# Hybrid attention and recurrence layer: the input norm's loads, squares, weight splits and first projection block in another order

## The chip, the cores and the metric

One Trainium2 chip, one core of it. The metric is the device time of one execution in microseconds, the median of the runs. A time belongs to the whole layer, of which the change touches the first part.

## The reference, cut to what matters

```
h = concat([meta (16 tokens), x (1024 tokens)])          # width 1024
a = rms_norm(h, norm_mix)                                # y = h * rsqrt(mean(h*h) + 1e-6) * g
(q_na, k_na, v_na, q_hg, z_f, z_b, i_hg, g_hg, gate_na, gate_hg) = split_cols(a @ w_in)
y_na = neighbourhood_attention(q_na, k_na, v_na) @ w_na_out
y_hg = hgrn2_branch(q_hg, z_f, z_b, i_hg, g_hg, lb, hg_norm) @ w_hg_out   # 4 heads of 128
h = h + (sigmoid(gate_na) * y_na + sigmoid(gate_hg) * y_hg) @ w_o
h = h + square(relu(rms_norm(h, norm_mlp) @ w_up)) @ w_down
out = rms_norm(h, norm_final)                            # meta tokens dropped
```

The recurrence of a head needs two gates of z_f and z_b, f = lb + (1 - lb) * sigmoid(z) and k = (1 - lb) * sigmoid(-z), where `lb` is the softmax over two rows of the input `hg_lb_logits`. All is float32.

## The kernel before

**Precision.** Each float32 matrix product is made of three matmuls on values that are split in a rounded part `hi` (fp32r) and a remainder `lo`: hi·hi, hi·lo, lo·hi (`mm3`, L134 to L137). A split takes a cast on ScalarE (ACT) for `hi` and a subtract for `lo`, on VectorE (DVE) almost everywhere.

**Input norm** (`norm_transpose`, L99). The input is worked off in tiles of 128 tokens, `xt` 0 to 7, and one of the 16 meta tokens, `xm`. For a tile, ACT squares it and sums the squares (L105), GpSimd (POOL) makes of the sum the factor `rs` (L92, L93), DVE multiplies the tile by `rs` and by the norm's gains `g_bc`, broadcast to all partitions (L107, result `na`, three buffers), TensorE (PE) transposes it in eight pieces of 128x128 into two PSUM banks (L111), and of each bank ACT casts `hi` (L114) and DVE subtracts `lo` (L115) into `aT`. `aT[0]` holds tiles 0 to 3 and the meta tokens, `aT[1]` tiles 4 to 7. The tile of the meta tokens comes first, then 0 to 7, and each runs the whole way in the code before the next begins.

**Loads.** All go over the queue of SyncE (SP), L153 to L162: tile 0, `xm`, `g_bc`, tiles 1 and 2, the weight block C_ZF, tiles 3 to 7, the block C_ZB, then `gain`. A weight block is 1024 x 128 values, 512 KB (`load_block`, L118): `raw` by DMA (L123), `hi` by ACT (L125), `lo` by the engine `eng` (L126). For these first two blocks `eng` is GpSimd. `lt`, the logits of `lb`, is loaded after them (L168); its softmax stands at L170 to L177.

**Projections** (`proj_steps`, L200). One block of 128 columns of `w_in` against all tokens, in pieces: the first half of the tokens, then the second (512 columns). Where the meta tokens are wanted (`meta_evac`), the first half is two pieces, of 256 and of 256 + 16 = 272 columns. A piece is 8 x 3 = 24 matmuls into one PSUM bank of three (`mm_tile`, L87), and `evac` reads it.

**Gates** (`gates_of`, L250): two sigmoids on ACT of each piece and three multiplies on DVE into `T0`, `X0`, `Y`. Head 0 goes in the order C_ZF 256, C_ZF 272, C_ZB first half (L283), then the second halves of both. The tiles are taken from the pool `hp` of the recurrence, which is opened behind the input norm's pool `p0` (L502, L146).

**Recurrence** (`hgrn`, L290). Behind the block C_Q (`ev_q`: `q`, then `QQ`, on DVE) come scores of 32x32 pieces, `kd` against `q` (L374), then seven levels, each with its scores of `X` against `QQ` (L390); between two levels DVE makes the next `X` and multiplies `QQ` (L396, L397, L413). `between()` (L350), called at L391 behind the scores of each level, puts in one piece of the block C_I (values `V`: copy `vt`, transposes `vpt`, copy `V`, L326 to L330), then pieces of the next head's gates. The driver at L514 runs head after head.

**Order.** The code is written in program order; the framework's scheduler decides in which order the instructions of each engine stand, and adds the waits on semaphores. So matmuls of the projection stand among the transposes. Within one engine the order is then fixed.

## Time and profile before

| | |
|---|---|
| median of three runs | 1551.93 us (1550.94 to 1554.89) |
| profiled execution | 1550.2 us |
| its span, first to last instruction | 1548.4 us |
| instructions | 23448 |
| PE busy | 1502.1 us, 97% |
| DVE, ACT, POOL busy | 65%, 42%, 26% |
| slice 1 of 40 (38.7 us): PE busy | 6 tenths, 9 in nearly all others |
| HBM over the span | 125 GB/s |

All times of rows are from the profiled execution, which took 1550.2 us; the span lies 1.8 us below that. Read ahead of all else the slices: the only one in which PE is busy for clearly under nine tenths at the start of the program is the first, which is the input norm. "Idle before, releaser" in a row of the timeline is the time that the engine stood before the instruction, and whose event ended it. Starts are in us from the span's start. Matmuls are pipelined, so the spacing of their starts, not their duration, says how fast they follow each other.

### The profile page before, as it was taken

What the parts mean: (1) busy time and instruction counts of PE and PEld (TensorE: products, weight loads), DVE (VectorE), ACT (ScalarE), POOL (GpSimd) and SP (SyncE); (2) the same over time, 40 slices, a digit from 0 to 9 for tenths busy, and PEclk for the clock granted to TensorE, in tenths of its full rate; (3) what the DMA queues carried; (4) which work ended last, traced back from release to release, by engine and by line L of the source; (5) the groups of instructions that cost most, each with busy time, mean ns of one, the idle gap of its engine ahead of it and who ended that gap; (6) DMA issues with size and microseconds to landing.
All of it is one profiled execution on the core that took longest, in us unless ns stands there. A gap on an engine that the chain in (4) does not pass through costs nothing.

```text
span 1548.4 us, 23448 instructions
## 1 busy us (share of the span) xinstructions
PE 1502.1 (97%) x9188; PEld 1253.5 (81%) x9188; DVE 1008.4 (65%) x1592; ACT 654.7 (42%) x1168; POOL 401.8 (26%) x359
## 2 busy tenths in 40 slices
PE   6999999999999998999999999999999999999998
PEld 5788888878888887888888887888888788887886
DVE  6666666664876877666475369666666444879566
ACT  6231313124665666334122245555555433434444
POOL 4413131315315310011000032444444200237033
PEclk9999999999999999999999999999999999999999
DMA  5101010113123128434951324444444576563224
GB/s 181 43 28 56 28 56 28 55 29 128 49 72 119 55 69 272 136 123 163 339 178 41 109 91 148 165 155 153 153 150 148 169 273 233 190 231 107 98 82 150
DMA packets 142335, 195.61 MB, mean 126 GB/s; under 512 B 8064, under 2 KB 90112, under 8 KB 142224
## 3 DMA queue, kind: packets, MB, share of 16 engines
q1 hardware_dynamic: 133856, 173.40, 33.8%
q10 hardware_dynamic: 6192, 13.37, 2.2%
q0 software_dynamic: 2176, 7.34, 1.3%
q8 instruction: 72, 1.18, 0.3%
q14 instruction: 39, 0.32, 0.1%
HBM read 139.55 MB, written 54.53 MB: 125 GB/s over the span
## 4 chain that ended last, share of the span: by engine, by line
PE 83%; DVE 9%; issue 3%; ACT 2%; DMA 2%; POOL 1%; DVEq 0%; POOLq 0%; SPq 0%; ACTq 0%
PE mm L135 11%; PE mm L136 10%; PE mm L137 10%; PE mm L1112 4%; PE pa L1112 4%; PE pb L691 4%; PE pb L692 4%; PE pb L693 4%; PE pc L1112 4%; PE pb L1112 4%; PE pc L693 2%; PE pc L692 2%; PE pc L691 2%; PE pa L692 2%; PE pa L691 2%
## 5 line engine op out<-in xcount | busy, mean ns | idle before, releaser
L135 PE MATMUL mm<-aT,hi 128*128 128x512 f32 (+2 forms) x640 | 230.2, 360 | 2.7 <-DVE QX L563 1.5
L137 PE MATMUL mm<-aT,lo 128*128 128x512 f32 (+2 forms) x640 | 227.8, 356 | 0.0
L136 PE MATMUL mm<-aT,hi 128*128 128x512 f32 (+2 forms) x640 | 226.6, 354 | 0.0
L97 DVE TENSOR_TENSOR dl<-ur,dh 128x1024 fp32r<-128x1024 f32 x55 | 76.6, 1393 | 93.7 <-ACT dh L96 93.5
L135 PEld LDWEIGHTS mm<-aT,hi 128*128 128x128 f32 x640 | 121.9, 191 | 17.2 <-issue 1.7
L137 PEld LDWEIGHTS mm<-aT,lo 128*128 128x128 f32 x640 | 121.8, 190 | 13.5 <-POOL lo L126 0.3
L136 PEld LDWEIGHTS mm<-aT,hi 128*128 128x128 f32 x640 | 121.9, 190 | 12.4
L96 ACT CAST dh<-ur 128x1024 fp32r<-128x1024 f32 x55 | 57.9, 1053 | 162.5 <-issue 78.1
L125 ACT CAST hi<-raw 128x1024 fp32r<-128x1024 f32 x36 | 37.8, 1051 | 106.7 <-PE mm L136 75.6
L974 ACT CAST wh<-sx 128x512 fp32r<-128x512 f32 x70 | 42.5, 618 | 94.7 <-DMA sx<-in_w_up 33.1
L975 DVE TENSOR_TENSOR wl<-sx,wh 128x512 fp32r<-128x512 f32 x70 | 51.2, 738 | 31.0 <-ACT wh L974 31.0
L975 DVE TENSOR_TENSOR wl<-raw,wh 128x512 fp32r<-128x512 f32 x46 | 50.2, 1090 | 23.7 <-ACT wh L974 22.9
L979 ACT ACTIVATE uv<-uv 128x512 f32<-128x512 f32 x48 | 30.4, 632 | 67.4 <-DVE uv L1090 50.0
L1095 POOL TENSOR_TENSOR us<-u,uv 128x512 f32<-128x512 f32 x15 | 24.0, 1603 | 133.4 <-ACT uv L980 133.4
L1202 POOL TENSOR_TENSOR w<-w,tt 128x512 f32<-128x512 f32 x16 | 23.3, 1458 | 134.0 <-DVE tt L1201 120.4
L399 POOL TENSOR_TENSOR Y<-X,TN 128x512 f32<-128x512 f32 x20 | 35.0, 1749 | 86.1 <-DVE X L396 86.1
L691 PE MATMUL pb<-nt,wh 128*128 128x512 f32 x128 | 50.4, 394 | 3.6 <-DVE uv L1083 2.6
L126 DVE TENSOR_TENSOR lo<-raw,hi 128x1024 fp32r<-128x1024 f32 x34 | 43.2, 1270 | 15.6 <-ACT hi L125 15.4
L92 POOL TENSOR_SCALAR rtm<-ssq 128x1 f32<-128x1 f32 (+1 forms) x17 | 6.4, 376 | 180.4 <-ACT junk L924 156.0
L618 DVE CUSTOM_DVE_ANT_0 pr<-nsc,NB 128x432 f32<-128x432 f32 (+1 forms) x64 | 35.2, 559 | 26.6 <-PE nsc L613 26.5
L1112 PE MATMUL mm<-dl,dh 128*128 128x512 f32 x126 | 49.9, 396 | 2.1 <-DVE dl L97 2.1
L135 PE MATMUL mm<-o,hi 128*128 128x512 f32 x128 | 50.0, 390 | 0.6 <-DVE mix L850 0.6
(380 smaller groups left out, 4409.3 us busy)
## 6 DMA issues: line engine op xcount, KB each, us to landing
raw<-in_w_in SPq DMA_DIRECT2D x56, 512.0 KB, 3.9
ur<-usp SPq DMA_DIRECT2D x55, 512.0 KB, 3.5
raw<-in_w_up SPq DMA_DIRECT2D x16, 1024.0 KB, 5.5
usp<-us SPq DMA_DIRECT2D x60, 256.0 KB, 2.0
sg<-gsp SPq DMA_DIRECT2D x16, 512.0 KB, 4.3
w<-in_w_dn SPq DMA_DIRECT2D x16, 512.0 KB, 4.5
usp<-uv SPq DMA_DIRECT2D x30, 256.0 KB, 2.2
gsp<-gv ACTq DMA_DIRECT2D x24, 256.0 KB, 2.4
```

What stands on the lines that cost most here:

```text
L96: act.copy(hi, src)
L97: dve.tensor_tensor(lo, src, hi.bitcast(F32), op=ALU.subtract)
L126: eng.tensor_tensor(lo[:, :kc], raw[:, :kc], hi[:, :kc].bitcast(F32), op=ALU.subtract)
L135: pe.matmul(ps, lh, rh, start=first, stop=False)
L136: pe.matmul(ps, lh, rl, start=False, stop=False)
L137: pe.matmul(ps, ll, rh, start=False, stop=last)
L691: pe.matmul(ps, lhs[0][:, c], rhs[0][:, k], start=first and k == 0, stop=False, skip_group_check=True)
L692: pe.matmul(ps, lhs[0][:, c], rhs[1][:, k], start=False, stop=False, skip_group_check=True)
L693: pe.matmul(ps, lhs[1][:, c], rhs[0][:, k], start=False, stop=k == 3, skip_group_check=True)
L974: act.copy(v(hi), src)
L975: dve.tensor_tensor(v(lo), src, v(hi).bitcast(F32), op=ALU.subtract)
L1112: pe.matmul(ps, a[n == 2][:, q, j * P:(j + 1) * P], b[n == 1][:, q], start=first and n == 0, stop=last and n == 2, skip_group_check=True)
```

## The change

- Loads: tile 0, `lt`, the block C_ZF, tile 1, `xm`, tiles 2 and 3, the block C_ZB, tiles 4 to 7, `gain` on SP's queue; `g_bc` is issued by ACT.
- The norm is cut in two functions: `norm_scale` (square and `rs`) and `norm_transpose` (multiply and what follows). The square of the next tile is written ahead of the multiply of this one. The meta tokens come third.
- The `lo` subtracts of C_ZF and C_ZB go from GpSimd to DVE.
- The softmax of `lt` is written ahead of the tiles.
- The gates' tiles come from a pool of their own, `hpg`, opened ahead of `p0`, which goes to the other side of SBUF; before, they lay in `hp`, behind `p0`.
- C_ZF of head 0 goes in pieces of 128, 128, 272 and 512 columns.
- In head 0, `between()` is called once more, ahead of the `kd` scores.

```diff
         act.copy(hi, src)
         dve.tensor_tensor(lo, src, hi.bitcast(F32), op=ALU.subtract)
-    def norm_transpose(sp_pool, src, g_bc, dst, c0, n, nbuf):
+    def norm_scale(sp_pool, src, n, nbuf):
         ssq = sp_pool.tile([P, 1], F32, tag="ssq", name="ssq", bufs=4)
         rs = sp_pool.tile([P, 1], F32, tag="rs", name="rs", bufs=4)
...
         a = sp_pool.tile([P, D], F32, tag="na", name="na", bufs=nbuf)
         act.activation(a[:n], src, AF.Square, accum_out=ssq[:n])
         rsqrt_mean(rs[:n], ssq[:n], D, tm[:n])
+        return rs, a
+    def norm_transpose(rs, a, src, g_bc, dst, c0, n):
         dve.scalar_tensor_tensor(a[:n], src, rs[:n], g_bc[:n], op0=ALU.mult, op1=ALU.mult)
         for j in range(2):
             pt = bank("a", "pt")
...
             dve.tensor_tensor(lo, pt[:, :, :n], hi.bitcast(F32), op=ALU.subtract)
-    def load_block(src, kc, scale=None, eng=dve):
+    def load_block(src, kc, scale=None):
         raw = wp.tile([P, KC, P], F32, tag="raw", name="raw")
         hi = wp.tile([P, KC, P], F32R, tag="hi", name="hi")
...
         sp.dma_start(raw[:, :kc], src.rearrange("(k p) c -> p k c", p=P))
         if scale is None:
             act.copy(hi[:, :kc], raw[:, :kc])
-            eng.tensor_tensor(lo[:, :kc], raw[:, :kc], hi[:, :kc].bitcast(F32), op=ALU.subtract)
+            dve.tensor_tensor(lo[:, :kc], raw[:, :kc], hi[:, :kc].bitcast(F32), op=ALU.subtract)
...
     aT = [u_tiles(h, "aT") for h in range(2)]
-    with tc.tile_pool(name="p0", bufs=1) as p0:
+    hgs = ExitStack()
+    hpg = hgs.enter_context(tc.tile_pool(name="hpg", bufs=1, reuse_waits="tile"))
+    with tc.tile_pool(name="p0", bufs=1, side="right") as p0:
         g_bc = p0.tile([P, D], F32, name="g_bc")
         xm = p0.tile([NM, D], F32, name="xm")
         xt = [p0.tile([P, D], F32, tag="xt", name="xt", bufs=8) for _ in range(8)]
+        lt = p0.tile([P, 2, 2, NHG], F32, name="lt")
         def load_x(i):
             sp.dma_start(xt[i], x[i * P:(i + 1) * P, :])
         load_x(0)
+        act.dma_start(g_bc, g_mix.rearrange("(o d) -> o d", o=1).broadcast_to([P, D]))
+        sp.dma_start(lt.rearrange("p a b c -> p (a b c)"), lbl)
+        early = {C_ZF: load_block(w_in[:, C_ZF:C_ZF + P], KC)}
+        load_x(1)
         sp.dma_start(xm, meta)
-        sp.dma_start(g_bc, g_mix.rearrange("(o d) -> o d", o=1).broadcast_to([P, D]))
-        load_x(1)
-        load_x(2)
-        early = {C_ZF: load_block(w_in[:, C_ZF:C_ZF + P], KC, eng=pool)}
-        for i in range(3, 8):
+        for i in range(2, 4):
             load_x(i)
-        early[C_ZB] = load_block(w_in[:, C_ZB:C_ZB + P], KC, eng=pool)
+        early[C_ZB] = load_block(w_in[:, C_ZB:C_ZB + P], KC)
+        for i in range(4, 8):
+            load_x(i)
         sp.dma_start(gain_sb, gain)
-        norm_transpose(p0, xm, g_bc, aT[0], TH, NM, 3)
-        norm_transpose(p0, xt[0], g_bc, aT[0], 0, P, 3)
-        for i in range(1, 8):
-            norm_transpose(p0, xt[i], g_bc, aT[i // 4], (i % 4) * P, P, 3)
-        lt = p0.tile([P, 2, 2, NHG], F32, name="lt")
-        sp.dma_start(lt.rearrange("p a b c -> p (a b c)"), lbl)
         mx = p0.tile([P, 2, NHG], F32, name="mx")
         dve.tensor_tensor(mx, lt[:, :, 0], lt[:, :, 1], op=ALU.max)
         pool.tensor_tensor(lt[:, :, 0], lt[:, :, 0], mx, op=ALU.subtract)
...
         dve.reciprocal(mx, mx)
         pool.tensor_tensor(lb_sb, lt[:, :, 0], mx, op=ALU.mult)
         pool.tensor_tensor(oml_sb, lt[:, :, 1], mx, op=ALU.mult)
+        rows = [(xt[i], aT[i // 4], (i % 4) * P, P) for i in range(8)]
+        rows.insert(2, (xm, aT[0], TH, NM))
+        scaled = norm_scale(p0, rows[0][0], P, 3)
+        for n, (src, dst, c0, m) in enumerate(rows):
+            cur = scaled
+            if n + 1 < len(rows):
+                scaled = norm_scale(p0, rows[n + 1][0], rows[n + 1][3], 3)
+            norm_transpose(*cur, src, g_bc, dst, c0, m)
...
     def block_of(col):
         return early.pop(col, None) or load_block(w_in[:, col:col + P], KC, -0.125 if C_QN <= col < C_KN else None)
-    def proj_steps(col, evac, meta_evac=None):
+    def proj_steps(col, evac, meta_evac=None, first=256):
         hi, lo = block_of(col)
...
         if meta_evac is not None:
-            pieces = [(0, 0, 256, 0, 0), (0, 256, 256 + NM, 256, NM)]
+            pieces = [(0, c, first, c, 0) for c in range(0, 256, first)] + [(0, 256, 256 + NM, 256, NM)]
             pieces = [(0, 0, TH, 0, 0)]
         pieces.append((1, 0, TH, TH, 0))
...
-    def gates_of(hd, hp, tiles):
-        T0 = hp.tile([P, 2, T], F32, tag="T0", name="T0")
-        X0 = hp.tile([P, T], F32, tag="X0", name="X0")
-        Y = hp.tile([P, T], F32, tag="Y", name="Y", bufs=2)
-        fm = hp.tile([P, NM], F32, tag="fm", name="fm", bufs=2)
-        km = hp.tile([P, NM], F32, tag="km", name="km", bufs=2)
+    def gates_of(hd, tiles):
+        T0 = hpg.tile([P, 2, T], F32, tag="T0", name="T0")
+        X0 = hpg.tile([P, T], F32, tag="X0", name="X0")
+        Y = hpg.tile([P, T], F32, tag="Y", name="Y", bufs=2)
+        fm = hpg.tile([P, NM], F32, tag="fm", name="fm", bufs=2)
+        km = hpg.tile([P, NM], F32, tag="km", name="km", bufs=2)
         tiles += T0, X0, Y, fm, km
         def gate(d):
...
             oml = oml_sb[:, d, hd:hd + 1]
             def ev(ps, t0, n):
-                sf, sn = (hp.tile([P, TH], F32, tag="gt", name=q, bufs=4) for q in ("sf", "sn"))
+                sf, sn = (hpg.tile([P, TH], F32, tag="gt", name=q, bufs=4) for q in ("sf", "sn"))
                 act.activation(sf[:, :n], ps, AF.Sigmoid)
                 act.activation(sn[:, :n], ps, AF.Sigmoid, scale=-1.0)
                 dve.tensor_scalar(T0[:, 1 - d, t0:t0 + n], sf[:, :n], oml, lb, op0=ALU.mult, op1=ALU.add)
...
                 dve.tensor_scalar(km, km, oml, None, op0=ALU.mult)
             return ev, (mev if d == 0 else None)
-        zf = proj_steps(C_ZF + hd * P, *gate(0))
+        zf = proj_steps(C_ZF + hd * P, *gate(0), first=256 if hd else P)
         zb = proj_steps(C_ZB + hd * P, *gate(1))
         if hd == 0:
-            for z in (zf, zf, zb):
+            for z in (zf, zf, zf, zb):
                 yield next(z)
         for z in (zf, zb):
             yield from z
...
                     next(more, None)
         yield
+        if hd == 0:
+            between()
...
                 sp.dma_start(lm[0].rearrange("p l t -> p (l t)"), lmask)
             return lm[0]
         tiles = [[] for _ in range(NHG + 1)]
-        ahead = [gates_of(hd, hp, tiles[hd]) for hd in range(NHG)] + [iter(())]
+        ahead = [gates_of(hd, tiles[hd]) for hd in range(NHG)] + [iter(())]
         list(ahead[0])
         prev = None
         for hd in range(NHG):
...
             next(cur)
             prev = cur
         list(prev)
+    hgs.close()
```

Three places in the order. First **DVE**, the start of its queue. `lo<-raw,hi` is the subtract of a weight block, `na` the multiply of a tile, `aT` the `lo` subtract of transposed tiles, `mx<-lt` and `mx<-mx` steps of the softmax. Before:

```order
L107 SCALAR_TENSOR_TENSOR na<-xm,rs,g_bc 16x1024
L107 SCALAR_TENSOR_TENSOR na<-xt,rs,g_bc 128x1024
L115 TENSOR_TENSOR aT_91<-pt,aT_90 128x4x16 x2
L107 SCALAR_TENSOR_TENSOR na<-xt,rs,g_bc 128x1024 x2
L115 TENSOR_TENSOR aT_91<-pt,aT_90 128x4x128 x3
L107 SCALAR_TENSOR_TENSOR na<-xt,rs,g_bc 128x1024
```

After:

```order
L176 TENSOR_TENSOR mx<-lt 128x8
L130 TENSOR_TENSOR lo<-raw,hi 128x1024
L111 SCALAR_TENSOR_TENSOR na<-xt,rs,g_bc 128x1024
L181 RECIPROCAL mx<-mx 128x8
L111 SCALAR_TENSOR_TENSOR na<-xt,rs,g_bc 128x1024
L111 SCALAR_TENSOR_TENSOR na<-xm,rs,g_bc 16x1024
L119 TENSOR_TENSOR aT_91<-pt,aT_90 128x4x128 x2
L111 SCALAR_TENSOR_TENSOR na<-xt,rs,g_bc 128x1024
L119 TENSOR_TENSOR aT_91<-pt,aT_90 128x4x128
L130 TENSOR_TENSOR lo<-raw,hi 128x1024
L119 TENSOR_TENSOR aT_91<-pt,aT_90 128x4x128
L119 TENSOR_TENSOR aT_91<-pt,aT_90 128x4x16 x2
```

The weight subtract of C_ZF now stands ahead of the first multiply, and that of C_ZB among those of the tiles.

Second **PE**, at the transposes of tile 7 (the last `pt<-ident,na`). The matmuls of 512 columns before are of C_ZB, those of 272 of C_ZF. Before:

```order
L135 MATMUL mm<-aT_90,hi 128x512
L136 MATMUL mm<-aT_91,hi 128x512
L111 MATMUL pt<-ident,na 128x128 x8
L137 MATMUL mm<-aT_90,lo 128x512
L135 MATMUL mm<-aT_90,hi 128x512
```

After:

```order
L141 MATMUL mm<-aT_90,lo 128x128
L139 MATMUL mm<-aT_90,hi 128x272
L115 MATMUL pt<-ident,na 128x128 x4
L140 MATMUL mm<-aT_91,hi 128x272
L115 MATMUL pt<-ident,na 128x128 x4
L141 MATMUL mm<-aT_90,lo 128x272
L139 MATMUL mm<-aT_90,hi 128x272
```

Before, eight matmuls of C_ZB stand ahead of the last transposes and 16 of its first half behind them; now two of the 272-column piece stand ahead of the last four transposes, and 22 of them and all of C_ZB behind.

Third **PE**, in head 0, at the `kd` scores (`sc<-q,kd`) and the first level's scores (`sc<-QQ,X`). The matmuls of 256 and 272 columns are the block C_I, `vpt` the transposes of its values. Before:

```order
L136 MATMUL mm<-aT_91,hi 128x256
L374 MATMUL sc<-q,kd 32x32 x16
L137 MATMUL mm<-aT_90,lo 128x256
L135 MATMUL mm<-aT_90,hi 128x256
L136 MATMUL mm<-aT_91,hi 128x256
L137 MATMUL mm<-aT_90,lo 128x256
L135 MATMUL mm<-aT_90,hi 128x272
L136 MATMUL mm<-aT_91,hi 128x272
L390 MATMUL sc<-QQ,X_386 32x32 x32
L329 MATMUL vpt<-ident,vt 128x128 x2
L137 MATMUL mm<-aT_90,lo 128x272
```

After:

```order
L141 MATMUL mm<-aT_90,lo 128x272
L139 MATMUL mm<-aT_90,hi 128x272
L345 MATMUL vpt<-ident,vt 128x128 x2
L392 MATMUL sc<-q,kd 32x32 x32
L408 MATMUL sc<-QQ,X_389 32x32 x32
L140 MATMUL mm<-aT_91,hi 128x272
```

The whole piece of 256 columns and 13 matmuls of the 272-column one now stand ahead of the `kd` scores, where before the second half of those scores stood among the 256s.

## Rows read from the trace of the kernel before

**Rows 1.** The page, part 1: busy us, share of the span, instructions.

```profile
PE 1502.1 (97%) x9188; PEld 1253.5 (81%) x9188; DVE 1008.4 (65%) x1592; ACT 654.7 (42%) x1168; POOL 401.8 (26%) x359
```

**Rows 2.** Waits of PE, 0 to 120 us: total us, times, longest us.

```profile
PE pt L111 <- DVE na L107: 11.0, 4, 10.0
PE pt L111 <- DVE aT L115: 3.6, 1, 3.6
```

**Rows 3.** Waits of DVE, 0 to 40 us.

```profile
DVE na L107 <- DMA g_bc<-in_g_mix: 8.6, 1, 8.6
DVE na L107 <- POOL rs L93: 4.0, 4, 1.6
```

**Rows 4.** Timeline, 0 to 40 us, SP, ACT, DVE, POOL: start, duration, engine, line, operation, tiles.

```profile
0.73 0.38 SPq L152 DMA_DIRECT2D xt<-in_x  x1
...
3.04 0.43 SPq L123 DMA_DIRECT2D raw<-in_w_in  x1
...
9.83 1.06 ACT L105 ACTIVATE na<-xt 128x1024 f32<-128x1024 f32 x1 [2.66 <-DMA xt<-in_x]
...
11.11 0.40 DVE L115 TENSOR_TENSOR aT<-pt,aT 128x64 fp32r<-128x64 f32 x2
...
13.93 2.35 POOL L126 TENSOR_TENSOR lo<-raw,hi 128x1024 fp32r<-128x1024 f32 x1
13.93 3.43 DVE L107 SCALAR_TENSOR_TENSOR na<-xt,rs,g_bc 128x1024 f32<-128x1024 f32 x1 [0.72 <-POOL rs L93]
...
27.38 1.28 DVE L115 TENSOR_TENSOR aT<-pt,aT 128x512 fp32r<-128x512 f32 x2
...
33.04 1.28 DVE L107 SCALAR_TENSOR_TENSOR na<-xt,rs,g_bc 128x1024 f32<-128x1024 f32 x1 [1.57 <-POOL rs L93]
```

**Rows 5.** Timeline of PE, 18 to 40 us (x4: four instructions in one row).

```profile
18.02 1.12 PE L111 MATMUL pt<-ident,na 128*128 128x128 f32 x4 [3.57 <-DVE aT L115]
...
22.98 0.41 PE L137 MATMUL mm<-aT,lo 128*128 128x256 f32 x1
23.20 0.42 PE L135 MATMUL mm<-aT,hi 128*128 128x256 f32 x1
...
27.59 0.29 PE L136 MATMUL mm<-aT,hi 128*128 128x272 f32 x1
27.71 0.29 PE L137 MATMUL mm<-aT,lo 128*128 128x272 f32 x1
...
34.47 1.17 PE L111 MATMUL pt<-ident,na 128*128 128x128 f32 x8 [0.67 <-DVE na L107]
...
35.71 0.39 PE L135 MATMUL mm<-aT,hi 128*128 128x512 f32 x1
...
39.13 0.39 PE L135 MATMUL mm<-aT,hi 128*128 128x512 f32 x1
```

**Rows 6.** Stretch of 10 to 15 us: length, then each engine's busy us.

```profile
10.00:15.00 5.00, 4.05 (x20) 3.17 (x20) 3.86 (x5) 4.83 (x11) 3.25 (x5) 1.00 1.06 414
```

**Rows 7.** DMA issued at 0.73 and 3.04 us: queue, KB each, us to landing.

```profile
xt<-in_x SPq DMA_DIRECT2D x1, 512.0 KB, 3.8
...
raw<-in_w_in SPq DMA_DIRECT2D x1, 512.0 KB, 9.6
```

**Rows 8.** Operations on `raw`, 0 to 60 us: ns min/median/max, first and last start.

```profile
L125 ACT CAST hi<-raw x4: 1050/1055/1066, 12.8 to 50.0; 128x1024 fp32r<-128x1024 f32 x4
...
L126 DVE TENSOR_TENSOR lo<-raw,hi x2: 1224/1225/1226, 45.6 to 51.1; 128x1024 fp32r<-128x1024 f32 x2
```

**Rows 9.** Timeline of PE in head 0.

```profile
61.63 0.39 PE L135 MATMUL mm<-aT,hi 128*128 128x256 f32 x1
...
66.73 0.46 PE L374 MATMUL sc<-q,kd 128*32 128x32 f32 x32 [2.44 <-DVE q L316]
...
72.39 0.77 PE L390 MATMUL sc<-QQ,X 128*32 128x32 f32 x64
```

**Rows 10.** Stretch of 68 to 72 us; granted clock behind POOL's column (0.57).

```profile
68.00:72.00 4.00, 3.77 (x78) 3.62 (x78) 3.05 (x6) 0.00 (x0) 0.00 (x0) 0.57 0.31 92
```

## The prediction

> **What bounds the kernel now.** I read the page's busy shares first. TensorE (PE) is busy for 1502.1 of 1548.4 us [rows 1], so all that a change of the opening can win is the time in which PE has nothing to do, or works at its lower clock; the rest is a queue of matmuls that only moves earlier or later as a whole. Then PE's waits up to 120 us [rows 2]: 11.0 us for the scaled rows `na` (10.0 of it ahead of its first instruction) and 3.6 us for an `aT` subtract, all in the opening; the next in size stands in head 0, of which more below. Behind that PE works through. So the question is at what time the same later matmul starts in each kernel, and I follow the chain to two such places.
>
> DVE is what PE waits for in the opening. Its waits [rows 3] are 8.6 us for the broadcast `g_bc`, then four times for `rs` of GpSimd (4.0 us). One multiply takes 3.43 us where the others take 1.28, and starts with the GpSimd subtract of 2.35 us [rows 4].
>
> The clock: at 23 us two matmuls of 256 columns start 0.22 us apart, at 27.6 us two of 272 columns 0.12 [rows 5]. So PE ran at 1.2 GHz up to 23 us and at 2.4 GHz by 27.6; the granted column says 1.00 even ahead of that [rows 6], and I go by the spacing there.
>
> **The change, part by part.** *Start of DVE's queue.* Before, its first multiply starts with the landing of `g_bc` (8.6 us [rows 3]). Now the weight subtract `lo` of block C_ZF stands ahead of all multiplies, so what counts is the landing of its `raw`. Today that is the fifth of the 512 KB transfers, issued at 3.04 and landed 9.6 us later, at 12.6; the third, x's tile 1, landed at 9.8 (the square that waits for it starts at 9.83); the first, tile 0, issued at 0.73, landed 3.8 us later, at 4.5 [rows 4, 7]. In the new order `raw` has tile 0 ahead of it and `g_bc` beside it, so again it is the third: at most 9.8. If `g_bc` did not slow it: 4.5 + (12.6 − 9.8) / 2 = 5.9. I take 8.8, near the upper row, since as many bytes go ahead. The cast (1.05 us [rows 8]) and then `lo` start at about 9.9 (7.0 to 10.9).
>
> The Trainium skill has a rule on this, in "DMA: Bandwidth & Descriptors", section "Issuing engines are not separate DMA queues": DMAs of different issuing engines share the same 16 DMA engines and interleave, and a second issuer only saves issue time. No run here shows two issuers in this stretch; by that rule the landing would lie at the 9.8 end and my sum would be 1 us higher.
>
> *DVE's queue to the last multiply.* From the order of the changed kernel stand there: 2 weight subtracts of 1.23 [rows 8], 8 multiplies of 128 rows and one of 16 at 1.28, 11 subtracts of 512 columns at 0.64, and two of 16 tokens, 0.20 each [rows 4]: 2.5 + 11.5 + 7.0 + 0.4 = 21.4 us. Waits: the square now runs a tile ahead, so the four waits for `rs` should mostly go; 0.8 us for what is left (0 to the old 4.0). The 2.15 us of the stretched multiply go with GpSimd's subtract, and 2.5 us of subtracts come onto DVE: these two cancel. The last multiply ends at 9.9 + 21.4 + 0.8 = 32.1 us, against 33.04 + 1.28 = 34.3 before [rows 4]: 2.2 us earlier.
>
> *What PE still has to do then.* Here the gain turns. Before, the last eight transposes start at 34.47, and behind them stand 16 of the 24 matmuls of C_ZB's first half; C_ZF's second half starts at 39.13 [rows 5]. In the changed order the last four transposes stand behind the second of 24 matmuls of the 272-column piece, with nothing of C_ZB begun: 22 × 0.125 + 24 × 0.228 = 8.2 us of matmuls (0.125 between the 272s, a shade over the 0.12 that the two rounded starts show; (39.13 − 35.71) / 15 = 0.228 for 512 [rows 5]). Transposes before took 1.17 us from 0.15 us after the multiply; the same now ends them at 33.4. C_ZF's second half then starts at 33.4 + 8.2 = 41.6, **2.5 us later** than today. The early matmuls that should have filled the opening can't: they lie in 128-column pieces among the transposes, and each next transpose waits for DVE (about 2.5 us a tile: 1.28 + 2 × 0.64).
>
> The 24 more matmuls of the first block (two of 128 columns for one of 256): each costs between 0.06 (half of the 0.12) and 0.15 (1.17 / 8, a transpose of that width) [rows 5]; less the 24 × 0.12 that go, 0 to 4.3 us. They are hidden by those waits for DVE, so I cost them at nothing; without that cover it is up to 4.3.
>
> *The clock in the opening.* PE starts later (about 12.5), with gaps. If the rise comes at about 24 to 28, as now, the transposes until then delay DVE's own subtracts; I cost 0.8 us (0 if it rises before 20; the rest of the bound is a rival).
>
> *Squares, gates' tiles, lower bounds.* ACT has the same instructions; the sigmoids of the first piece come between squares now, which frees a PSUM bank sooner, but PE did not wait for one [rows 2]: nothing. `lbl`'s small arithmetic moves ahead on GpSimd and DVE, two steps of 8 columns on DVE, each below the 0.20 of a subtract of 64 [rows 4]: nothing. On SP, C_ZB's `raw` and tiles 4 to 7 now queue behind the landing of `g_bc` (they share a completion semaphore), but six transfers of 512 KB stand ahead of them on the DMA engines anyway: nothing, as long as tile 7 lands before 25 us.
>
> *The piece that is moved into head 0.* Today PE goes from its first C_I matmul, at 61.63, to the second level's scores, at 72.39, in 10.8 us, of which it waits 2.44 at one place [rows 9] and has the lower clock for part: a mean of 0.57 granted in 68 to 72 us [rows 10], so (1 − 0.57) × 4 = 1.7 us lost, 3.4 us at half speed. The chain there is DVE's: q, QQ, V, X, two more QQ. The same chain stands in the changed kernel, so I take the same 10.8 us. What differs is what PE gets done meanwhile: 9 more 272-column matmuls and 2 of 512, 9 × 0.125 + 2 × 0.228 = 1.6 us. So 1.6 us are won, not the 2.44: the wait moves from the `kd` scores to the scores of the next level. The chain could also shorten (by the 2.44 of wait and the 1.7 us of the lower clock, 4.1 in all). And PE still stands for some 3 us, so the clock may fall again, then behind the chain, where it costs up to 1.7. I take half: −1.6 + 0.8 = −0.8.
>
> **Sum**: +2.5 + 0.8 − 0.8 = **+2.5 us**. The profiled execution took 1550.2 us (span 1548.4), the median of the three runs is 1551.93, 1.7 us more. Added to the median: **1554.4 us**. About 0.3% (4.7 us) is what a measurement of this kernel tells from no change: 1547.3 and 1556.6 are the bounds.
>
> **The rivals.** *The clock stays low until the dense part* (slower). The rise came behind 23.2 us; PE's work was unbroken only from 18.02 on, its wait of 3.57 us. In 10 to 15 us PE was busy for 4.05 of 5 us, with transposes alone, and at 23 us the clock was still low [rows 5, 6]. Now nothing dense comes before the last transposes at 33.4. Then the first 3.4 us (as long as the fall in head 0 lasted) to 5.2 us (18.0 to 23.2) of dense work, or somewhat more, go at half speed, 1.7 to 3.0 us lost, and the doubled transposes (1.17 us for eight, then 2.3) no longer hide in DVE's 2.5 us a tile, about 1.2 more. In place of my 0.8 that gives +2.9 to 4.2, and with the second fall of the clock (0.8 more) +2.5 − 0.8 + 3.5 + 0.8 = +6.0: 1557.9. It decides when the clock rises only after about 33 us. [...] Against it: at the low clock PE has few gaps left, as it had none from 18 us.
>
> *An early start* (no change). `raw` lands at 5.9 rather than 8.8: all of the opening moves by up to 2.9, so +2.5 − 2.9 − 0.8 + 0.8 = −0.4, and with no second fall −1.2; 1551. For it: tile 0 needs 3.8 us. Against it: between 3 and 10 us today's transfers did not keep that pace (tiles 0 and 1 landed 5.3 us apart, with two transfers between).
>
> *The moved piece fills head 0's wait wholly* (faster). The early start, and the wait and the low clock in head 0 both gone: 2.5 − 2.9 − 4.1 = −4.5, with neither 0.8 left in it: 1547.4. Against it: the chain of DVE has the same instructions.
>
> *The change doesn't do what it says*: the squares ahead still wait, so that `rs` is late as before, +3.2 on the sum: 1557.6. ACT has no fewer instructions; but each square now stands ahead of the casts that wait for PE.
>
> **How the numbers follow.** The forecast case (1552 to 1556.6) 0.50; the early start 0.18 (1549.5 to 1552); the clock 0.17 and the squares 0.05, nearly all beyond 1556.6; the faster one 0.10, most of it at or past 1547.3. Faster 0.08, same 0.70, slower 0.22. The range leaves out the fast rival and the far end of the slow ones (a fall of the clock and no cover for the 24 matmuls): 1549.5 to 1559.0.
>
> **What would show it.** In the changed profile: the first `lo` on DVE at 9.9 us and the first transposes near 12.5 (before 10.0); no multiply above 1.3 us; the last transposes done by 33.4; no 512-column matmul before them, and C_ZF's second half near 41.6 (39.13). In head 0, no wait ahead of the `kd` scores, but one of 2 to 3 us ahead of the scores of the level behind. From head 1 on both kernels have the same order, so the difference there should stay what it is at 120 us. I am wrong if the last transposes come before 30 us, if 512-column matmuls start before them, or if the wait in head 0 is gone.

## The result and the profile after

The changed kernel takes 1556.8 us (median of 14 runs, 1554.65 to 1559.32) where the kernel before takes 1551.24 (14 runs, 1545.99 to 1556.05): a ratio of 1.0037, 95% interval 1.0027 to 1.0046, so between 4.2 and 7.1 us slower. The forecast was 1554.4, within 1549.5 to 1559.0: the direction holds, the size was 2.5 us and is 5.6, and the case "slower by over 0.3%", to which I gave 0.22, is the one that came. A ratio and its interval are estimated from all runs of both kernels and are not the quotient of the two medians. One run of experiment 8 took 1867.84 us and is left out of its ratio. The profiled execution took 1559.32 us, its span is 1557.5.

Busy times answer to [rows 1]; PE has 24 matmuls more.

```profile
PE 1509.1 (97%) x9212; PEld 1260.0 (81%) x9212; DVE 1012.7 (65%) x1597; ACT 655.9 (42%) x1170; POOL 396.0 (25%) x357
```

PE's waits, 0 to 120 us, in the profile after (total us, times, longest us), answer to [rows 2] and to the 2.44 us of [rows 9]: the wait of head 0 now stands at the second level's scores (L408), at 79.25 us.

```profile
PE pt L115 <- DVE na L111: 13.5, 4, 12.3
PE pt L115 <- DVE aT L119: 3.1, 2, 1.8
PE sc L408 <- DVE QQ L431: 2.9, 1, 2.9
```

DVE's waits, 0 to 45 us, answer to [rows 3]. The wait for `rs` is halved, not gone, and two new ones stand beside it: for ACT's casts, and 0.9 us for a step of the softmax.

```profile
DVE lo L130 <- ACT hi L129: 3.6, 2, 3.2
DVE aT L119 <- ACT aT L118: 2.2, 3, 1.5
DVE na L111 <- POOL rs L93: 1.9, 2, 1.1
DVE mx L181 <- POOL mx L180: 0.9, 1, 0.9
```

PE's timeline, 20 to 46 us (start, duration, operation, tiles). Up to 23.5 us narrow matmuls start 0.21 us apart, and tile 2's transposes come at 23.50. At 27.3 us they start 0.11 apart. The last four transposes start at 37.42, nothing of C_ZB stands ahead of them, and C_ZF's second half starts at 46.10, 7.0 us later than the 39.13 of [rows 5].

```profile
20.21 0.41 PE L139 MATMUL mm<-aT,hi 128*128 128x128 f32 x1
20.42 0.41 PE L140 MATMUL mm<-aT,hi 128*128 128x128 f32 x1
...
23.50 1.93 PE L115 MATMUL pt<-ident,na 128*128 128x128 f32 x8
...
27.29 0.28 PE L140 MATMUL mm<-aT,hi 128*128 128x128 f32 x1
27.40 0.28 PE L141 MATMUL mm<-aT,lo 128*128 128x128 f32 x1
...
33.02 1.03 PE L115 MATMUL pt<-ident,na 128*128 128x128 f32 x4 [1.26 <-DVE aT L119]
...
37.42 0.60 PE L115 MATMUL pt<-ident,na 128*128 128x128 f32 x4
37.77 0.37 PE L141 MATMUL mm<-aT,lo 128*128 128x272 f32 x1
...
46.10 0.39 PE L139 MATMUL mm<-aT,hi 128*128 128x512 f32 x1
```

The granted clock in three stretches of five us (the number behind POOL's column): it had risen by 27 us and fell again at about 33, and once more in head 0.

```profile
30.00:35.00 5.00, 3.23 (x21) 3.12 (x22) 4.28 (x6) 3.94 (x9) 1.70 (x4) 0.81 0.01 3
35.00:40.00 5.00, 5.00 (x39) 5.00 (x38) 4.39 (x11) 2.77 (x6) 0.00 (x0) 0.84 0.00 0
80.00:85.00 5.00, 5.00 (x63) 4.01 (x61) 2.97 (x6) 0.00 (x0) 1.53 (x1) 0.66 0.01 3
```

Two marks serve below. The first is the start of C_ZF's second half, which ends the opening. The second is the first state update of head 0 on DVE (`SF`), at 111.91 us before and 118.69 after; behind it both kernels have the same order, and the 6.8 us between them stay what they are to 460 us (within 0.2). The ends of the two spans, 9.1 us apart, are no measure: between 460 and 1050 us the profiles part by 1 to 4 us at several places, in kernels that have the same order there. Part of it is the clock, which in some falls and in others doesn't (in 960 to 980 us granted 0.91 after, 1.00 before). The marks come from the one profiled run of a kernel, the medians from all; where they disagree, the text says so.

### The profile page after: what moved, and what is told of

Its sections match the earlier page's. It is cut to its first block, busy times and chain, and to the rows that moved or that the text cites. A ratio compares the mean times of both kernels' runs of the same rounds, so it can differ in the third digit from the quotient of the medians.

```text
span 1557.5 us, 23494 instructions
## 1 busy us (share of the span) xinstructions
PE 1509.1 (97%) x9212; PEld 1260.0 (81%) x9212; DVE 1012.7 (65%) x1597; ACT 655.9 (42%) x1170; POOL 396.0 (25%) x357
## 4 chain that ended last, share of the span: by engine, by line
PE 84%; DVE 8%; DMA 3%; issue 2%; ACT 1%; POOL 1%; SPq 0%; DVEq 0%; POOLq 0%; ACTq 0%
PE mm L139 11%; PE mm L140 10%; PE mm L141 10%; PE mm L1131 4%; PE pa L1131 4%; PE pb L710 4%; PE pb L711 4%; PE pb L712 4%; PE pc L1131 4%; PE pb L1131 4%; PE pc L710 3%; PE pc L711 3%; PE pc L712 3%; PE pa L710 2%; PE pa L711 2%
## 5 line engine op out<-in xcount | busy, mean ns | idle before, releaser
L139 PE MATMUL mm<-aT,hi 128*128 128x512 f32 (+3 forms) x648 | 232.5, 359 | 2.1 <-DVE QX L582 1.5
L141 PE MATMUL mm<-aT,lo 128*128 128x512 f32 (+3 forms) x648 | 230.6, 356 | 0.0
L140 PE MATMUL mm<-aT,hi 128*128 128x512 f32 (+3 forms) x648 | 229.6, 354 | 0.0
L139 PEld LDWEIGHTS mm<-aT,hi 128*128 128x128 f32 x648 | 124.0, 191 | 16.3 <-issue 1.7
L140 PEld LDWEIGHTS mm<-aT,hi 128*128 128x128 f32 x648 | 123.9, 191 | 12.8
```

The source lines that it names most:

```text
L139: pe.matmul(ps, lh, rh, start=first, stop=False)
L140: pe.matmul(ps, lh, rl, start=False, stop=False)
L141: pe.matmul(ps, ll, rh, start=False, stop=last)
```

## The experiments

What is called narrow is a matmul of 128 columns. All experiments change the changed kernel ("after") or the kernel before. Medians stand against runs of the kernel before on the same chip.

**1. The narrow pieces undone.**

```diff
-        zf = proj_steps(C_ZF + hd * P, *gate(0), first=256 if hd else P)
+        zf = proj_steps(C_ZF + hd * P, *gate(0), first=256)
...
-            for z in (zf, zf, zf, zb):
+            for z in (zf, zf, zb):
```

> The changed kernel with the first block of head 0 in the pieces of before (256, 272, 512 columns) instead of 128, 128, 272, 512. Marks: the start of C_ZF's second half (39.13 us before, 46.10 after) and the first state update of head 0 on DVE (111.91 before, 118.69 after). Theory A, the narrow pieces: in the profile after, a matmul of 128 columns takes 0.21 us at the lower clock, as one of 256 columns does before, so the 24 extra cost about 24 x 0.21 at the lower clock, 3 us of it ahead of tile 2's transposes (done 4 us after its multiply). Then C_ZF's second half starts at 41 to 42.5, the state update at 113 to 115, and the median is 3 to 5 us below the changed kernel's. Theory B, DVE, ACT and the clock set the pace and PE's extra matmuls fit in its gaps: second half no earlier than 45, median within 1.5 us of the changed kernel's.

PE's timeline of this kernel: the second matmul of C_ZB (its first stands alone at 27.55), the last transposes, and the first matmul of C_ZF's second half. Then PE's waits, 0 to 120 us; 12.3 of them lie ahead of its first instruction.

```profile
33.33 0.39 PE L140 MATMUL mm<-aT,hi 128*128 128x512 f32 x1
...
36.07 1.15 PE L115 MATMUL pt<-ident,na 128*128 128x128 f32 x8
...
40.47 0.39 PE L139 MATMUL mm<-aT,hi 128*128 128x512 f32 x1
```

```profile
PE pt L115 <- DVE na L111: 12.6, 2, 12.3
...
PE pt L115 <- DVE aT L119: 2.6, 3, 1.9
```

Second half at 40.47 (the 40.69 that the later expectations quote is its second matmul), state update at 114.10, median 1550.66 against 1552.13 (0.9989, 0.9978 to 1.0001): theory A. By the medians the whole loss of the change is gone with this one part; by the state update 4.6 of 6.8 us. One half of the theory did not hold: tile 2's transposes still start late, at 23.21, since eleven matmuls of 256 columns now stand ahead of them, and at the lower clock those take the same 0.21 us. The gain comes behind: nine matmuls of C_ZB are done ahead of the last transposes, where after begins C_ZB at 40.60, behind them. DVE is no faster: its last multiply ends at 35.91 (35.35 after).

**2. The moved piece in head 0 undone.**

```diff
         yield
-        if hd == 0:
-            between()
```

> The changed kernel without the piece of C_I that is moved ahead of the kd scores of head 0; the opening is the same. Theory: this part alone wins in head 0 (the offset to before falls from 7.0 us at C_ZF's second half to 6.8 or less at the state update), so without it the state update comes 0.8 to 1.6 us later than in the changed kernel (119.5 to 120.3), with the 2.4 us wait of PE ahead of the kd scores back. Rival: the wait only changes its place (2.89 us ahead of the next scores), and the state update stays within 0.4 us of 118.7.

PE's waits of this kernel, 55 to 100 us:

```profile
PE sc L390 <- DVE q L332: 2.6, 2, 2.4
```

The wait is back at its old place (2.4 us behind `q`), and the state update comes at 118.50, with a second half at 45.64: 72.86 us between the marks, where after has 118.69 − 46.10 = 72.59. The moved piece wins 0.3 us here, not 0.8. Median 1557.6 against 1552.13 (1.0037, 1.0023 to 1.0050). The rival holds.

**3. The gates' tiles behind the rows again.**

```diff
-    hpg = hgs.enter_context(tc.tile_pool(name="hpg", bufs=1, reuse_waits="tile"))
-    with tc.tile_pool(name="p0", bufs=1, side="right") as p0:
+    with tc.tile_pool(name="p0", bufs=1) as p0:
...
+    hpg = hgs.enter_context(tc.tile_pool(name="hpg", bufs=1, reuse_waits="tile"))
     with tc.tile_pool(name="hp", bufs=1, reuse_waits="tile") as hp:
```

> The changed kernel with the gates' tiles behind the input norm's again (one pool, opened after it), so that no sigmoid and no table load stand among the squares and casts. Theory C: in the profile after, ACT loads the sigmoids' table at 29.13 us (1.28 us) and runs one sigmoid, in the middle of the tiles; the casts behind it start at 30.59, DVE waits 0.72 for rs, PE 1.26 for DVE, and the clock falls at 33 us for 3.5 us. Without it the last multiply ends 1.3 to 2.5 us earlier (33 to 34 instead of 35.35), no low clock after 30 us, and C_ZF's second half starts 1.5 to 4 us earlier (42 to 44.6). Rival: the sigmoids only take idle time of ACT, and they free a PSUM bank; second half within 0.7 us of 46.1, or later.

First ACT's timeline of after, where the sigmoids' table is loaded among the tiles; then, of this kernel, where it isn't, DVE's last multiply and PE's first matmul of C_ZF's second half.

```profile
29.13 1.28 ACT L281 ACT_TABLE_LOAD   x1
...
30.59 1.07 ACT L118 CAST aT<-pt 128x512 fp32r<-128x512 f32 x2
```

```profile
33.71 1.28 DVE L111 SCALAR_TENSOR_TENSOR na<-xt,rs,g_bc 128x1024 f32<-128x1024 f32 x1
```

```profile
44.43 0.39 PE L139 MATMUL mm<-aT,hi 128*128 128x512 f32 x1
```

C_ZF's second half 1.7 us earlier than after (44.43), state update at 116.91, a granted clock of 1.00 from 30 to 45 us, median 1555.61 against 1552.13 (1.0020, 1.0010 to 1.0030). One half of theory C holds, at the low end of its numbers: no low clock, and the second half earlier. The other doesn't: the last multiply ends at 34.99, 0.4 us earlier than after's 35.35, where 1.3 to 2.5 were expected. So most of the 1.7 us is PE's work at the higher clock and not a faster DVE. That the table load is what brought the clock down in after is argued from the order of events, not shown apart.

**4. Work for PE ahead of the first transposes.**

```diff
+    wt = bank("b", "warm")
+    for _ in range(32):
+        pe.matmul(wt[:, 0], ident, ident, start=True, stop=True)
     half_c = cp.tile([P, 8], F32, name="half")
```

> The changed kernel with 32 matmuls of the identity by itself (128 columns) at the start of PE's queue, from about 1.3 us, into a PSUM bank that nothing reads. It asks what the lower clock of the opening costs. Theory: the clock is up when the first transposes come at 12.3 us, eight take 1.2 us instead of 2.0, narrow matmuls 0.11 instead of 0.21, tile 2's transposes start near 20.5 instead of 23.5, and C_ZF's second half 3 to 4.5 us earlier (41.5 to 43). Rival 1: DVE and ACT set the pace, the lower clock is only a sign of PE's gaps; second half 0 to 1.5 us earlier. Rival 2: the clock falls again in the gap between the extra matmuls and the first transposes or in the gaps behind; the transposes at 12.3 still take 1.97 and nothing changes.

PE's timeline of this kernel (the trace has two records for each of the 32 matmuls), and two of its stretches:

```profile
1.35 8.93 PE L83 MATMUL warm<-ident 128*128 128x128 f32 x64 [1.35 <-POOL ident masks.py:199]
12.62 1.09 PE L118 MATMUL pt<-ident,na 128*128 128x128 f32 x8 [2.34 <-DVE na L114]
```

```profile
15.00:20.00 5.00, 2.44 (x10) 1.85 (x10) 4.03 (x5) 3.42 (x6) 1.50 (x5) 0.50 1.04 384
20.00:25.00 5.00, 5.00 (x27) 4.69 (x27) 2.92 (x6) 3.09 (x7) 1.17 (x3) 0.50 0.43 129
```

The clock was up for tile 0: its eight transposes take 1.09 us instead of 1.97. Then PE stands for 1.17, 0.45 and 2.11 us, the granted clock is 0.50 from 15 to 25 us, and the second half starts at 46.26: the second outcome of rival 2, though not its transposes of 1.97. An early start of PE does not keep the clock up here: it is low again behind these waits. The median is 1560.21 against 1552.13 (1.0048, 1.0034 to 1.0063), more than after's though both marks are nearly the same; its profile, the slowest of its six runs, loses the rest behind 500 us. The two intervals overlap; whether the extra work has a part in it stays open.

**5. Three parts undone together**: experiments 1 and 3, and the softmax written behind the tiles.

```diff
-        mx = p0.tile([P, 2, NHG], F32, name="mx")
...
             norm_transpose(*cur, src, g_bc, dst, c0, m)
+        mx = p0.tile([P, 2, NHG], F32, name="mx")
...
```

> The changed kernel with three parts undone together: the pieces of 128 columns (256 again), the gates' tiles beside the rows (behind them again), and the softmax written ahead of the tiles (behind them; its load stays early). Left of the change: the loads on two queues, the weight subtracts on DVE, the meta tokens third, the piece moved in head 0. Alone, the first gave 5.4 us at the start of C_ZF's second half (46.10 to 40.69), the second 1.7 (to 44.43); the reciprocal of the softmax costs DVE 0.9 us of waiting. Theory, they add up: second half at 38.0 to 39.3, first state update at 111 to 113, median 6 to 8 us below the changed kernel's. Rival, without the narrow pieces DVE's own queue sets the end and the others are hidden: second half at 40 or later, median within 1 us of the first experiment's.

DVE's waits of this kernel, 0 to 45 us:

```profile
DVE aT L119 <- ACT aT L118: 2.9, 4, 1.8
```

Second half at 40.01, state update at 112.52, median 1551.3 against 1551.06 (1.0005, 0.9991 to 1.0019): the rival. With the narrow pieces gone, the other two give 0.46 us and not 2.6; DVE still waits for ACT's casts, 2.9 us in all. What is left of the change is not harmless: experiment 10 has the subtracts on DVE and the moved piece too, in the old order of loads and tiles, and its second half starts at 36.90. So the new order of the loads and of the meta tokens costs 3.1 us at this mark; which of its parts does was not tried, beyond `g_bc` in experiment 6.

**6. Before, with `g_bc` on ACT's queue alone.**

```diff
         load_x(0)
+        act.dma_start(g_bc, g_mix.rearrange("(o d) -> o d", o=1).broadcast_to([P, D]))
         sp.dma_start(xm, meta)
-        sp.dma_start(g_bc, g_mix.rearrange("(o d) -> o d", o=1).broadcast_to([P, D]))
```

> The kernel before with one part of the change: g_bc is issued by ACT behind tile 0, all else in the old order. In the profile after, g_bc landed 5.5 us after its issue at 0.72, at 6.2, and 8.6 before. Theory 1: the first multiply starts 1.2 to 1.6 us earlier (7.0 to 7.4, when rs of the meta tokens is there) and that carries through DVE's queue: C_ZF's second half at 37.5 to 38.2 (39.13 before), median 1 to 1.5 us below before. Theory 2: the third multiply waits for tile 1's landing (9.8) and its rs (11.9) as before, or for a later landing, since g_bc's bytes go ahead of tile 1's: the gain is gone there, second half within 0.5 us of 39.1, median the same.

Three of its loads (queue, KB, us from issue to landing), and the start of its tiles on GpSimd and DVE:

```profile
g_bc<-in_g_mix ACTq DMA_DIRECT2D x1, 512.0 KB, 5.7
xt<-in_x SPq DMA_DIRECT2D x1, 512.0 KB, 5.4
...
xm<-in_meta SPq DMA_DIRECT2D x1, 64.0 KB, 5.8
```

```profile
8.21 0.18 POOL L92 TENSOR_SCALAR rtm<-ssq 16x1 f32<-16x1 f32 x1 [6.91 <-ACT na L105]
...
9.06 1.27 DVE L107 SCALAR_TENSOR_TENSOR na<-xm,rs,g_bc 16x1024 f32<-16x1024 f32 x1 [9.06 <-POOL rs L93]
...
9.25 1.14 POOL L92 TENSOR_SCALAR rtm<-ssq 128x1 f32<-128x1 f32 x1 [0.23 <-ACT na L105]
```

`g_bc` landed 5.7 us after its issue instead of 6.9, but tile 0 took 5.4 instead of 3.8 [rows 7], and the 64 KB of the meta tokens 5.8. Their `rs` is late, the first multiply starts at 9.06, 0.4 us later than before, and the gain of theory 1 turns into a loss. The order that follows is another too; PE has a lower clock in 30 to 40 us (0.81 and 0.85 granted), and the second half starts at 42.67. One thing in it: both weight subtracts on GpSimd now meet a multiply (at 15.07 and 28.25 us, 3.36 and 3.40 us long), where before only one does. How the 3.5 us divide is not shown. Median 1553.96 against 1551.06 (1.0025, 1.0012 to 1.0037): slower, which neither theory had.

**7. Experiment 5 with the weight subtracts on GpSimd.**

```diff
-        early = {C_ZF: load_block(w_in[:, C_ZF:C_ZF + P], KC)}
+        early = {C_ZF: load_block(w_in[:, C_ZF:C_ZF + P], KC, eng=pool)}
```

(and the same for C_ZB)

> As the kernel with the three parts undone, and the weight subtracts of C_ZF and C_ZB back on GpSimd. It weighs the split of weights on DVE alone. Theory: the first subtract is what DVE's queue begins with (at 9.8 us, behind the landing of raw and its cast), so on GpSimd DVE begins with tile 0's multiply at 8.1 to 8.6 and has 2.5 us less to do, of which some 2.2 come back as a stretched multiply; C_ZF's second half 0.5 to 2.5 us earlier than in that kernel. Rival: GpSimd holds up rs (2.3 to 3.4 us for a subtract there against 1.23 on DVE) and DVE's multiply beside it, and the second half is 0.5 to 2 us later.

GpSimd's and DVE's timeline of this kernel at the start of the tiles:

```profile
9.64 2.34 POOL L130 TENSOR_TENSOR lo<-raw,hi 128x1024 fp32r<-128x1024 f32 x1 [8.35 <-ACT hi L129]
...
13.07 1.08 POOL L93 TENSOR_TENSOR rs<-rtm,half 128x1 f32<-128x1 f32 x2
...
13.66 2.48 DVE L111 SCALAR_TENSOR_TENSOR na<-xt,rs,g_bc 128x1024 f32<-128x1024 f32 x2 [7.10 <-POOL rs L93]
```

The subtract stands ahead of `rs` in GpSimd's queue, so the first multiply comes at 13.66 instead of 10.84. Second half at 40.94 (40.01 in experiment 5), median 1552.78 against 1551.06 (1.0017, 1.0004 to 1.0029). The rival, by the mark: in the new load order the subtract belongs on DVE. The medians alone don't tell the two kernels apart; their intervals overlap.

**8. Before, with the moved piece alone.**

```diff
         yield
+        if hd == 0:
+            between()
```

> The kernel before with one part of the change: the piece of C_I ahead of the kd scores in head 0. The opening is that of before, so C_ZF's second half, at 39.13 there, also shows how well an opening repeats (expected within 0.3 us). Theory, from the second experiment (where undoing it moved the state update by 0.3 us at most): PE's wait only moves to the next scores, and the clock falls behind it; state update within 0.5 us of 111.9, median the same as before. My forecast's step was a gain of 0.8 (between 0 and 1.6): state update at 111.1.

PE's waits in 55 to 100 us, and the stretch of 60 to 90:

```profile
PE sc L391 <- DVE QQ L414: 3.0, 1, 3.0
```

```profile
60.00:90.00 30.00, 26.76 (x526) 23.44 (x525) 24.21 (x42) 5.48 (x13) 11.26 (x10) 1.00 0.13 37
```

The opening repeats within 0.5 us (39.62). The state update comes at 110.71, 71.09 us behind the first mark (72.78 before): 1.7 us won, but with a granted clock of 1.00 in head 0, where before has 0.94 and loses 0.06 × 30 = 1.8 us. Median 1549.82 against 1551.06 (0.9997, 0.9980 to 1.0015): the same.

**9. Before, with the narrow pieces alone.**

```diff
-            pieces = [(0, 0, 256, 0, 0), (0, 256, 256 + NM, 256, NM)]
+            pieces = [(0, c, first, c, 0) for c in range(0, 256, first)] + [(0, 256, 256 + NM, 256, NM)]
```

(with `first` as in the change)

> The kernel before with one part of the change: C_ZF of head 0 in pieces of 128, 128, 272 and 512 columns. It asks from the other side what the narrow pieces cost. Theory A: a matmul of 128 columns follows the last one after 0.21 us at the lower clock and 0.11 at the higher, like one of 256 (0.21 and 0.12), so 24 more of them are 2.7 to 5.1 us of PE's time ahead of the last transposes; C_ZF's second half at 42 to 44.5 (39.13 and 39.62 in two profiles of that opening), median 2.5 to 5 us above before. Rival: in the old order PE's gaps ahead of the last transposes (4.3 us of waits behind the first transposes) take most of it; second half at 39.5 to 41, median within 1.5 us of before.

PE's timeline of this kernel: the last transposes, and the first matmul of C_ZF's second half. Then PE's waits, 0 to 120 us; 9.8 of them lie ahead of its first instruction.

```profile
31.84 1.06 PE L111 MATMUL pt<-ident,na 128*128 128x128 f32 x8 [1.76 <-DVE na L107]
...
42.14 0.39 PE L135 MATMUL mm<-aT,hi 128*128 128x512 f32 x1
```

```profile
PE pt L111 <- DVE na L107: 12.3, 4, 9.8
...
PE pt L111 <- DVE aT L115: 1.7, 2, 1.3
```

The last transposes come 2.6 us earlier than before (34.47 in [rows 5]), and still C_ZB begins 6.0 us later (at 36.65, 30.61 before) and the second half 3.0 us later, at 42.14. Median 1556.43 against 1549.91 (1.0037, 1.0024 to 1.0050): theory A, and by the median as much as the whole change. The marks say less: the state update comes at 114.09, 2.2 us behind that of before, the very time of experiment 1, whose median is no longer than before's. The profiled run is the fastest of seven here and the slowest of ten there; what parts the two kernels behind this mark was not found. So that the narrow pieces cost time is shown from both sides; how much of the 5.6 us they are is not.

**10. Before, with the weight subtracts on DVE and the moved piece.**

```diff
-        early = {C_ZF: load_block(w_in[:, C_ZF:C_ZF + P], KC, eng=pool)}
+        early = {C_ZF: load_block(w_in[:, C_ZF:C_ZF + P], KC)}
```

(the same for C_ZB, and `between()` as in experiment 8)

> The kernel before with two parts of the change, the ones that the runs so far speak for: the weight subtracts of C_ZF and C_ZB on DVE, and the piece of C_I ahead of the kd scores. The weight subtract stands in the old order behind tile 1's multiplies, not ahead of all. Theory: the stretched multiply (3.43 instead of 1.28) and the late rs of tile 7 (1.57) go, 2.46 us of subtracts come onto DVE; the last multiply ends 0.5 to 1.5 us earlier than in before (34.3; 34.8 in the second profile of that opening), C_ZF's second half at 37.7 to 38.7, state update at 109 to 111.5 (110.71 with the moved piece alone), median 1 to 2.5 us below before. Rival: DVE's queue is as long as before (2.46 more against 2.15 less) and the waits for rs come back as waits for ACT's casts; second half within 0.5 us of 39.4, median within 1 us of before.

C_ZF's second half on PE, and the stretch of 60 to 90 us:

```profile
36.90 0.49 PE L135 MATMUL mm<-aT,hi 128*128 128x512 f32 x1 [0.31 <-ACT sn L266]
```

```profile
60.00:90.00 30.00, 26.76 (x510) 22.97 (x510) 21.67 (x40) 4.21 (x12) 9.10 (x9) 0.89 0.13 37
```

The opening is 2.2 us shorter than before, more than expected, but head 0 takes 110.70 − 36.90 = 73.80 us, with a granted clock of 0.89 (3.3 us lost). Median 1549.66 against 1549.91 (0.9992, 0.9980 to 1.0004): the same.

**11. Before, with the weight subtracts on DVE alone.**

```diff
-        early[C_ZB] = load_block(w_in[:, C_ZB:C_ZB + P], KC, eng=pool)
+        early[C_ZB] = load_block(w_in[:, C_ZB:C_ZB + P], KC)
```

(and the same for C_ZF)

> The kernel before with one part of the change: the weight subtracts of C_ZF and C_ZB on DVE. With the moved piece in head 0 as well, the run before this one had C_ZF's second half at 36.90 us (39.13 and 39.62 in two profiles of the old opening), but the state update only at 110.71, since the clock fell behind PE's 3.0 us wait in head 0 (granted 0.94, 0.50 and 0.87 in 65 to 80 us, 3.4 us lost; the kernel before loses 1.7 there). Theory: the opening's gain is real and the moved piece is what puts it at risk; with head 0 as before the state update comes at 109 to 110 (111.91 before), median 1.5 to 3 us below before. Rival: head 0 is bound by DVE's chain behind q, whatever the opening won, or the fall of the clock comes here too; state update at 110.5 or later, median within 1 us of before.

DVE's timeline of this kernel: the multiply of tile 2, with 1.28 us instead of the 3.43 of [rows 4]; the weight subtract follows it at 15.54. Then PE's: C_ZF's second half.

```profile
14.34 1.28 DVE L107 SCALAR_TENSOR_TENSOR na<-xt,rs,g_bc 128x1024 f32<-128x1024 f32 x1 [0.72 <-POOL rs L93]
```

```profile
36.47 0.50 PE L135 MATMUL mm<-aT,hi 128*128 128x512 f32 x1 [0.31 <-ACT sn L266]
```

Second half at 36.47, state update at 109.06, median 1548.7 against 1551.92 (12 and 17 runs; 0.9982, 0.9969 to 0.9995). By its interval this kernel is faster than before, and after is slower than before. The gain is small beside what the reference itself does: the runs of before that stood beside experiments 9 and 10 have a median of 1549.91, on the same chip. And the same opening with the moved piece (experiment 10) kept nothing of it that shows.

Squares one tile ahead have no experiment: with `norm_scale` called in its old place the instructions of every engine stand in the same order as in the changed kernel. The scheduler had already chosen that order; the edit in the source does nothing.

## Why the prediction was right, and where its sum failed

Right here means that the time lies in the range and on the forecast side. The size does not: 2.5 us were forecast and 5.6 came, in the case "slower", which had 0.22. The range reached so far up because it allowed for the 24 matmuls without cover (up to 4.3 us); the sum itself had them at nothing. The direction came from a mechanism that held, the order behind the last transposes; that the time still lies in the range is in part luck, since two steps of the sum failed, both the same way.

| step | forecast | after |
|---|---|---|
| first weight subtract on DVE | 9.9 us | 9.85 |
| last multiply ends | 32.1 | 35.35 |
| last transposes done, 22 matmuls of 272 columns begin | 33.4 | 37.77 |
| these and C_ZB's first half | 8.2 | 8.33 |
| C_ZF's second half | 41.6, with the clock 42.4 | 46.10 |
| head 0, against before | −0.8 | −0.2 |

**Start of DVE's queue.** Right: `raw` landed at 8.7 (8.8 taken). The Trainium skill's rule, in "DMA: Bandwidth & Descriptors", section "Issuing engines are not separate DMA queues", has DMAs of two issuers interleave on the same 16 DMA engines. Experiment 6 agrees: tile 0's 512 KB took 5.4 us instead of 3.8 once `g_bc` went beside it. The later landing of 9.8 that I worked out from that rule did not come.

**What PE still has to do behind the last transposes.** Right in kind and size: no matmul of 512 columns ahead of them, 8.33 us of work behind. This is the mechanism that I had singled out. What failed is when this work begins: 37.77 instead of 33.4, of which 3.3 us lie ahead of the end of DVE's last multiply and 1.1 behind it.

**The 24 more matmuls: the step that failed.** I bounded each by 0.06 to 0.15 us, scaled with its columns and taken from rows at the higher clock, and costed them at nothing since DVE's pace would hide them. They follow each other after 0.21 us at the lower clock and 0.11 at the higher, as those of 256 and 272 columns do (0.22 and 0.12 [rows 5]). Between 128 and 256 columns a matmul has one price here. So 24 more are 24 × 0.21 = 5.0 us at the lower clock, 2.6 at the higher.

Nor were they hidden. PE's time up to C_ZF's second half can be divided into its start, its waits behind that, and the rest, which is work:

| | start | waits | work | second half |
|---|---|---|---|---|
| before | 10.0 | 4.6 | 24.5 | 39.1 |
| after | 12.3 | 4.3 | 29.5 | 46.1 |
| after, narrow pieces undone (1) | 12.3 | 2.9 | 25.3 | 40.5 |
| before, narrow pieces alone (9) | 9.8 | 4.2 | 28.1 | 42.1 |

Of the 7.0 us, 2.4 are the later start (2.5 forecast) and 5.0 more work; the waits, which were to shrink by what the matmuls fill, are 0.3 shorter. With the narrow pieces undone 4.2 us of work go, and alone they bring 3.6. Part of this price stood in my sum all the same, as the 8.2 us that the order leaves behind the last transposes.

The rows of PE's weight loads in after show what else stands there at 27 us (start, duration):

```profile
27.12 0.19 PEld L139 LDWEIGHTS mm<-aT,hi 128*128 128x128 f32 x1
27.23 0.19 PEld L140 LDWEIGHTS mm<-aT,hi 128*128 128x128 f32 x1
```

The loads follow each other at the matmuls' spacing, there and at the lower clock (20.10 and 20.32), and the loads' column in 20 to 25 us is busy for 4.84 of 5 us. That the loads set the price is suggested by this, not shown apart. The Trainium skill has a price for a load: "TensorE: Matmul & The Clock Gate", section "LDWEIGHTS (loading the stationary operand)", gives the number of its columns divided by 1.2 in ns, by estimate 0.107 us for 128. The trace agrees at the higher clock (0.11); at the lower the spacing is 0.21, and there the measurement decides.

**Waits of DVE.** I left 0.8 us; the profile has, from the first subtract to the last multiply, 0.90 for the softmax's reciprocal, 1.15 and 0.72 for `rs`, and 0.38 + 1.52 + 0.16 for casts of ACT, 4.8 in all. This is the other step that failed: with it the last multiply ends 3.3 us late. Of these waits, 1.52 stand behind tile 2:

```profile
18.08 1.26 DVE L111 SCALAR_TENSOR_TENSOR na<-xt,rs,g_bc 128x1024 f32<-128x1024 f32 x1
...
34.07 1.28 DVE L111 SCALAR_TENSOR_TENSOR na<-xt,rs,g_bc 128x1024 f32<-128x1024 f32 x1
```

its multiply ends at 19.34 and its transposes start at 23.50. The narrow matmuls ahead of them are not the cause: in experiment 1, with matmuls of 256 columns there, DVE waits 1.29 at this place. Two more things I had costed at nothing: the sigmoids among the squares, with their table load (1.7 us at the mark by experiment 3, though only 0.46 together with the softmax where the narrow pieces are gone), and the softmax ahead of the tiles (the 0.90).

**The clock.** 0.8 us was my term. The granted clock lost 5 × 0.19 + 5 × 0.16 = 1.75 us in 30 to 40 us. The rival "stays low until the dense part" had the place wrong: the clock rose at about 26 us, behind an unbroken row of narrow matmuls, and fell at 33, behind waits of 0.60 and 1.26 us. Its 1557.9 is near the measured median, but for another reason.

**The squares rival** (1557.6) named what came about, in part: `rs` was still late, 1.9 us of the old 4.0, and writing the squares ahead changed no order. It is not what made the time: before has more of that wait.

**Head 0.** The mechanism was right: the wait moved to the second level's scores (2.89 us, 2 to 3 forecast), and the clock fell behind it (0.66 granted in 80 to 85 us). The size was off. Ordered by the clock that the stretch of 60 to 90 us was granted, the time between the two marks reads:

| granted, 60 to 90 us | moved piece in | moved piece not in |
|---|---|---|
| 1.00 | 71.09 (exp. 8) | 71.95 (exp. 9) |
| 0.94 | 72.59 (after), 72.48 (3), 72.41 (4), 72.51 (5) | 72.78 (before), 72.86 (2), 72.77 (6), 72.59 (11) |
| 0.89 | 73.63 (1), 73.88 (7), 73.80 (10) | |

The piece is worth 0.3 us in the middle row and, by one profile each, 0.9 in the first, where I had 1.6 less 0.8. From row to row it is 0.8 to 1.4 us more, a little less than the 0.06 × 30 = 1.8 and 0.05 × 30 = 1.5 us of clock that are lost. What decides how long the clock stays down was not found: after and experiment 1 have the same wait there (2.9 and 3.0 us) and lose 1.8 and 3.3 us.

**The same difference from head 1 on.** Right up to 460 us; behind that single profiles differ by their own loads and clock.

## What to carry to other kernels

Count matmuls, not columns: with fp32r operands, and a weight load for each, a matmul of 128 columns here costs what one of 256 costs, so a cut into narrower pieces buys an earlier start at the price of a full slot per extra matmul, and the slot is twice as dear where the clock is low. An edit that moves work ahead in the source has to be read in the order of the instructions: the squares had not moved at all, and the sigmoids brought their table load in among the tiles. Of a change in seven parts try the parts alone; here one of them, the subtract off GpSimd, was worth some 0.2%, and one lost twice that, by the medians.
